# Gathered embeddings plus positions on one core: the first four sequences gathered by halves, with half of the positions and the later indices loaded behind the first half

## The chip, the cores and the metric

The kernel runs on one core of one Trainium2 chip. The metric is the device time of one execution in microseconds (us); lower is better. The program was run several times per measurement, and the median is given. Where a kernel was timed against the kernel before, the two ran alternately on the same chip. Three chips took part in the experiments, and one of them shows a longer closing of the program, which is described where it matters.

## The reference

```python
batch, seq_len, vocab_size, d_model = 32, 512, 50000, 512
def reference(indices, embedding_table, position_embed):
    token_embed = embedding_table[indices]          # (32, 512, 512) float32
    return (token_embed + position_embed).astype(np.float32)
```

There are 16,384 rows of 2 KB to fetch, one position row to add to each, and 33.6 MB to write. Indices come as 64-bit integers.

## The kernel before

A sequence of 512 rows lies on 128 partitions with K = 4 rows each, so a "gather" (one indirect DMA issued from GpSimd) fetches 128 rows, 256 KB. The 128 gathers are numbered by g. VectorE adds the positions, which ScalarE has copied to PSUM, and SyncE stores half sequences (512 KB); the first and the last sequence are stored in quarters.

```python
SLOTS = 24; LANES = 16                       # buffers of a whole sequence; semaphores of gathers
# SyncE: the loads, all issued at once
nc.sync.dma_start(out=idx0[:], in_=idx_first).then_inc(s_first, 16)       # indices of sequence 0: 4 KB
nc.sync.dma_start(out=idx_raw[:], in_=...).then_inc(s_raw, 16)            # all indices: 128 KB
for k in range(K):
    nc.sync.dma_start(out=pos_sb[k][:], in_=pos_rows[:, k, :]).then_inc(s_pos[k], 16)   # 4 x 256 KB
# GpSimd: the gathers
nc.gpsimd.wait_ge(s_first, 16)
for g in range(B * K):
    b, k = divmod(g, K)
    if g == K:
        nc.gpsimd.wait_ge(s_idx, 1)          # later indices, turned by TensorE
    ...
    where = idx0[:, 2 * k : 2 * k + 1] if b == 0 else idx_t[:, k, b : b + 1]
    ins = nc.gpsimd.indirect_dma_start(out=slots[b % SLOTS][:, k, :], out_offset=None,
        in_=table, in_offset=bass.IndirectOffsetOnAxis(ap=where, axis=0),
    ).then_inc(s_gather[g % LANES], 16)
# VectorE: one add for each gather, in the same order; waits for s_gather (and s_ps for b == 0)
# SyncE: stores, each waits for its adds
for b, at, n in stores:
    nc.sync.dma_start(out=out_rows[b][:, at : at + n, :], in_=slots[b % SLOTS][:, at : at + n, :],
    )._wait_ge(s_add, b * K + at + n).then_inc(done, 16)
```

Of the kernel before, what the change touches and what calls it, by code (L numbers as in the profile page):

```python
# [1 line left out]

# [4 lines left out]

P = 128
K = 4
SLOTS = 24  # L10
LANES = 16
HALVES = (2, 2)
QUARTERS = (1, 1, 1, 1)


@with_exitstack
def kernel(
    ctx: ExitStack,
    tc: tile.TileContext,
    indices: bass.AP,  # L20
    embedding_table: bass.AP,
    position_embed: bass.AP,
    out: bass.AP,
):




    nc = tc.nc
    f32 = mybir.dt.float32  # L30
    i32 = mybir.dt.int32
    add = mybir.AluOpType.add

    B, S = indices.shape
    V, D = embedding_table.shape
    assert S == P * K and B == 32
    assert V < (1 << 24), "an index passes through float32"


    idx_words = indices.bitcast(i32)  # L40
    idx_first = idx_words[0].rearrange("(p w) -> p w", p=P)
    out_rows = out.rearrange("b (p k) d -> b p k d", k=K)
    pos_rows = position_embed.rearrange("(p k) d -> p k d", k=K)
    table = embedding_table[:, :]

    def sbuf(name, shape, dtype):
        return ctx.enter_context(tc.tile_pool(name="p_" + name, bufs=1)).tile(
            shape, dtype, name=name
        )

    def psum(name, shape, dtype):
        pool = tc.tile_pool(name="p_" + name, bufs=1, space=bass.MemoryType.PSUM)
        return ctx.enter_context(pool).tile(shape, dtype, name=name)

    idx0 = sbuf("idx0", [P, 2 * K], i32)
    idx_raw = sbuf("idx_raw", [B, S, 2], i32)
    ones = sbuf("ones", [B, B], f32)
    ident = sbuf("ident", [B, B], f32)
    idx_f = sbuf("idx_f", [B, P, K], f32)
    idx_t = sbuf("idx_t", [P, K, B], i32)  # L60
    pos_sb = [sbuf(f"pos_sb{k}", [P, D], f32) for k in range(K)]
    slots = [sbuf(f"slot{n}", [P, K, D], f32) for n in range(SLOTS)]
    turned = psum("turned", [P, K, B], f32)
    pos_ps = [psum(f"pos_ps{k}", [P, D], f32) for k in range(K)]


    stores = []
    for b in range(B):
        parts = QUARTERS if b in (0, B - 1) else HALVES
        at = 0  # L70
        for n in parts:
            stores.append((b, at, n))
            at += n

    sem = tc.alloc_semaphore
    s_first, s_raw = sem("s_first"), sem("s_raw")
    s_pos = [sem(f"s_pos{k}") for k in range(K)]
    s_gather = [sem(f"s_gather{n}") for n in range(LANES)]

    s_out = {b: sem(f"s_out{b}") for b in range(B - SLOTS)}  # L80
    s_rest = sem("s_rest")
    s_ident, s_cast, s_turn, s_idx, s_ps, s_add = (
        sem(n) for n in ("s_ident", "s_cast", "s_turn", "s_idx", "s_ps", "s_add")
    )

    def rounds(g):
        return 16 * (g // LANES + 1)

    with tc.tile_critical(no_gpsimd_drain=True):  # L89

        nc.sync.dma_start(out=idx0[:], in_=idx_first).then_inc(s_first, 16)
        nc.sync.dma_start(
            out=idx_raw[:], in_=idx_words.rearrange("b (s w) -> b s w", w=2)
        ).then_inc(s_raw, 16)
        for k in range(K):
            nc.sync.dma_start(out=pos_sb[k][:], in_=pos_rows[:, k, :]).then_inc(
                s_pos[k], 16
            )


        nc.gpsimd.memset(ones[:], 1.0).then_inc(s_ident, 1)  # L101
        nc.gpsimd.affine_select(  # L102
            out=ident[:], in_=ones[:], pattern=[[-1, B]],
            compare_op=mybir.AluOpType.is_equal, fill=0.0, base=0,
            channel_multiplier=1,
        )._wait_ge(s_ident, 1).then_inc(s_ident, 1)
        nc.gpsimd.wait_ge(s_first, 16)
        for g in range(B * K):
            b, k = divmod(g, K)
            if g == K:  # L110
                nc.gpsimd.wait_ge(s_idx, 1)
            if b >= SLOTS and k == 0:
                done = sum(1 for x in stores if x[0] == b - SLOTS)
                nc.gpsimd.wait_ge(s_out[b - SLOTS], 16 * done)  # L114
            where = idx0[:, 2 * k : 2 * k + 1] if b == 0 else idx_t[:, k, b : b + 1]
            ins = nc.gpsimd.indirect_dma_start(  # L116
                out=slots[b % SLOTS][:, k, :],
                out_offset=None,
                in_=table,
                in_offset=bass.IndirectOffsetOnAxis(ap=where, axis=0),  # L120
            ).then_inc(s_gather[g % LANES], 16)
            if g >= LANES:
                ins._wait_ge(s_gather[g % LANES], rounds(g - LANES))
        nc.gpsimd.drain()  # L124


        nc.tensor.wait_ge(s_ident, 2)
        for k in range(K):
            ins = nc.tensor.transpose(turned[:, k, :], idx_f[:, :, k], ident[:])  # L129
            ins.then_inc(s_turn, 1)  # L130
            if k == 0:
                ins._wait_ge(s_cast, 1)


        nc.vector.tensor_copy(  # L135
            out=idx_f[:].rearrange("b p k -> b (p k)"), in_=idx_raw[:, :, 0]
        )._wait_ge(s_raw, 16).then_inc(s_cast, 1)
        nc.vector.tensor_copy(out=idx_t[:], in_=turned[:])._wait_ge(  # L138
            s_turn, K
        ).then_inc(s_idx, 1)  # L140
        for g in range(B * K):
            b, k = divmod(g, K)
            if b == 0:
                nc.vector.wait_ge(s_ps, k + 1)
            part = slots[b % SLOTS][:, k, :]
            nc.vector.tensor_tensor(  # L146
                out=part, in0=part, in1=pos_ps[k][:], op=add
            )._wait_ge(s_gather[g % LANES], rounds(g)).then_inc(s_add, 1)


        for k in range(K):
            nc.scalar.copy(out=pos_ps[k][:], in_=pos_sb[k][:])._wait_ge(  # L152
                s_pos[k], 16
            ).then_inc(s_ps, 1)
        rest = 0
        for b, at, n in stores:
            done = s_out.get(b, s_rest)
            rest += done is s_rest
            nc.sync.dma_start(
                out=out_rows[b][:, at : at + n, :],  # L160
                in_=slots[b % SLOTS][:, at : at + n, :],
            )._wait_ge(s_add, b * K + at + n).then_inc(done, 16)
        nc.sync.wait_ge(s_rest, 16 * rest)


# [1 line left out]
_INS = ['indices', 'embedding_table', 'position_embed']  # L167
_OUTS = [((32, 512, 512), 'float32')]


# [23 lines left out]
```

## Time and profile before

| quantity | before | where it is read |
|---|---|---|
| time | 177.56 us (177.3 to 177.7, 4 runs) | runs |
| span of the profiled run | 175.4 us | the page |
| bytes moved | 68.33 MB | the page |
| GpSimd's first and last gather issued | 2.88 and 162.23 us | the timeline |
| interval between issues, after the first 30 | 1.2526 us | the timeline |
| last byte moved | 173.18 us | the trace's DMA packets |

The page of the kernel before. The row DMA gives the busy share of the 16 DMA engines in tenths in 40 slices of 4.4 us, GB/s what they moved. A group's line ends with busy time, mean ns of one, idle time and what ended it.

```profile
DMA  3989999999999999999999999999999999999993
GB/s 110 305 251 325 406 405 370 406 398 412 408 407 417 392 419 419 418 419 418 416 419 419 418 417 418 419 417 419 417 417 419 417 419 419 415 413 416 419 413 139
...
L116 POOL DMA_INDIRECT slot<-in_embedding_table_dram,idx_t x124 | 117.5, 948 | 37.8 <-issue 37.8
L146 DVE TENSOR_TENSOR slot<-slot,pos_ps 128x512 f32<-128x512 f32 x128 | 87.8, 687 | 77.1 <-DMA slot<-in_embedding_table_dram,idx_t 72.8
```

From 61 us on, every slice but the last shows 413 to 419 GB/s, about 418 in the mean. That is a gather and an equal share of a store, 524,288 bytes, each 1.2526 us: 418.6 GB/s. So GpSimd's issue rate and the flow of bytes agree. VectorE is idle half of the time.

The waits of the kernel before (who waited for what: us in total, times, longest):

```profile
POOL slot L116 <- issue: 38.7, 127, 0.3
...
POOL slot L116 <- DMA idx<-in_indices_dram: 1.5, 1, 1.5
```

GpSimd waits for no other engine and no buffer after the first indices. "Issue" is 0.30 us between two gathers that nothing in the profile explains.

Windows of the kernel before. The last two columns count: the busy share of the DMA engines, and GB/s. The share is the summed time of the packets that start in the window, over 16 engines, and can come out slightly above 1.

```profile
core 0: us, PE busy (x) PEld busy (x) DVE busy (x) ACT busy (x) POOL busy (x), PEclk, DMA share, GB/s
...
2.50:4.00 1.50, 0.00 (x0) 0.00 (x0) 0.00 (x0) 0.00 (x0) 1.12 (x1) 1.00 0.89 253
4.00:6.00 2.00, 0.68 (x4) 0.55 (x4) 0.70 (x2) 0.59 (x1) 1.39 (x3) 1.00 0.79 215
...
10.00:12.00 2.00, 0.00 (x0) 0.00 (x0) 2.00 (x4) 0.00 (x0) 1.39 (x3) 1.00 0.78 204
12.00:14.00 2.00, 0.00 (x0) 0.00 (x0) 0.81 (x2) 0.00 (x0) 1.70 (x2) 1.00 0.99 358
14.00:16.00 2.00, 0.00 (x0) 0.00 (x0) 0.69 (x1) 0.00 (x0) 1.39 (x3) 1.00 1.02 290
16.00:20.00 4.00, 0.00 (x0) 0.00 (x0) 1.88 (x3) 0.00 (x0) 3.08 (x4) 1.00 0.98 378
20.00:40.00 20.00, 0.00 (x0) 0.00 (x0) 10.39 (x16) 0.00 (x0) 15.12 (x17) 1.00 1.02 395
...
60.00:80.00 20.00, 0.00 (x0) 0.00 (x0) 11.00 (x16) 0.00 (x0) 15.12 (x17) 1.00 1.03 415
...
164.00:168.00 4.00, 0.00 (x0) 0.00 (x0) 2.06 (x3) 0.00 (x0) 0.00 (x0) 1.00 1.03 421
```

The first 20 us move less than the later ones.

The end of the chain of waits (start us, us, what), and the landing times of gathers issued from 80 to 160 us:

```profile
162.23 7.47 DMA slot<-in_embedding_table_dram,idx_t
169.70 0.02 issue
169.72 0.69 DVE slot L146
```

```profile
DMA to landing us min/median/max: 6.9/7.3/7.8
```

A gather takes 7.3 us to land in mid-run and 7.47 us at the end. The shortest landing in this trace is 4.4 us. The last add comes at 169.72 us, and the last byte at 173.18 us, 10.96 us after GpSimd's last issue.

The first add:

```profile
9.50 2.63 DVE L146 TENSOR_TENSOR slot<-slot,pos_ps 128x512 f32<-128x512 f32 x4 [3.93 <-DMA slot<-in_embedding_table_dram,idx]
```

### The profile page before, as it was taken

Reading aid. Unit: us, or ns where it says so; the run is one execution under the profiler, and the core shown is the slowest. Engines: PE = TensorE matmul, PEld = TensorE weight load, DVE = VectorE, ACT = ScalarE, POOL = GpSimd, SP = SyncE. Lnnn points to the kernel's source line nnn. Section 1 sums busy time; section 2 is a strip of 40 time slices with the busy share of each in tenths; the row PEclk is TensorE's granted clock in tenths of the full one; section 3 lists DMA queues with packets and bytes.
Section 4 is the critical chain, followed back from the end, with each engine's and each line's share of the span. In section 5 each row is a group of like instructions: output and inputs, shape, how many; then the busy total and the mean of one; then the engine's idle time right before and its main releaser. Section 6 shows DMA issues by size and latency. Waiting matters only on the chain.

```text
span 175.4 us, 421 instructions
## 1 busy us (share of the span) xinstructions
PE 0.7 (0%) x4; PEld 0.6 (0%) x4; DVE 88.5 (50%) x130; ACT 3.6 (2%) x5; POOL 122.1 (70%) x134
## 2 busy tenths in 40 slices
PE   0100000000000000000000000000000000000000
PEld 0100000000000000000000000000000000000000
DVE  0072564564646455554655555555554546556440
ACT  2410000000000000000000000000000000000000
POOL 3777777777777777777777777777777777777200
DMA  3989999999999999999999999999999999999993
GB/s 110 305 251 325 406 405 370 406 398 412 408 407 417 392 419 419 418 419 418 416 419 419 418 417 418 419 417 419 417 417 419 417 419 419 415 413 416 419 413 139
DMA packets 20803, 68.33 MB, mean 390 GB/s; under 512 B 3360, under 2 KB 3360, under 8 KB 20800
## 3 DMA queue, kind: packets, MB, share of 16 engines
q1 hardware_dynamic: 10560, 34.74, 49.4%
q0 software_dynamic: 10240, 33.56, 49.1%
q14 instruction: 3, 0.02, 0.1%
HBM read 34.74 MB, written 33.55 MB: 389 GB/s over the span
## 4 chain that ended last, share of the span: by engine, by line
POOL 67%; issue 24%; DMA 5%; POOLq 1%; DVE 0%; SPq 0%
POOL slot L116 67%; DMA slot<-in_embedding_table_dram,idx_t 4%; DMA idx<-in_indices_dram 1%; POOLq L124 1%; DVE slot L146 0%; POOLq L114 0%; SPq L189 0%; SPq L89 0%
## 5 line engine op out<-in xcount | busy, mean ns | idle before, releaser
L116 POOL DMA_INDIRECT slot<-in_embedding_table_dram,idx_t x124 | 117.5, 948 | 37.8 <-issue 37.8
L146 DVE TENSOR_TENSOR slot<-slot,pos_ps 128x512 f32<-128x512 f32 x128 | 87.8, 687 | 77.1 <-DMA slot<-in_embedding_table_dram,idx_t 72.8
L116 POOL DMA_INDIRECT slot<-in_embedding_table_dram,idx x4 | 4.0, 1009 | 2.4 <-DMA idx<-in_indices_dram 1.5
L135 DVE CAST idx_f<-idx_raw 32x512 f32<-32x512 int32 x1 | 0.4, 414 | 4.1 <-DMA idx_raw<-in_indices_dram 4.1
L152 ACT COPY pos_ps<-pos_sb 128x512 f32<-128x512 f32 x4 | 2.4, 589 | 4.8 <-DMA pos_sb<-in_position_embed_dram 4.6
L152 ACT ACT_TABLE_LOAD x1 | 1.3, 1283 | 1.0 <-SPq L89 1.0
L129 PE MATMUL turned<-ident,idx_f 32*128 32x32 f32 x4 | 0.7, 308 | 4.6 <-DVE idx_f L135 4.6
L138 DVE CAST idx_t<-turned 128x128 int32<-128x128 f32 x1 | 0.3, 291 | 0.8 <-PE turned L129 0.8
L129 PEld LDWEIGHTS turned<-ident,idx_f 32*128 32x128 f32 x4 | 0.6, 206 | 4.6 <-DVE idx_f L135 4.6
L101 POOL MEMSET ones<- 32x32 f32 x1 | 0.1, 115 | 0.5 <-SPq L89 0.5
L178 POOL MEMSET const-float32-0.0<- 128x1 f32 x1 | 0.1, 105 | 0.3 <-issue 0.3
L102 POOL TENSOR_SCALAR_AFFINE_SELECT ident<-ones 32x32 f32<-32x32 f32 x1 | 0.2, 203 | 0.1
L178 POOL MEMSET const-uint8-127<- 128x1 uint8 x1 | 0.1, 122 | 0.0
L178 POOL MEMSET const-bfloat16-1.0<- 128x1 bf16 x1 | 0.1, 116 | 0.0
L178 POOL MEMSET const-float32-1.0<- 128x1 f32 x1 | 0.1, 108 | 0.0
## 6 DMA issues: line engine op xcount, KB each, us to landing
out_dram<-slot SPq DMA_DIRECT2D x60, 512.0 KB, 6.7
out_dram<-slot SPq DMA_DIRECT2D x8, 256.0 KB, 4.3
slot<-in_embedding_table_dram,idx_t POOLq DMA_INDIRECT x124, 7.2
pos_sb<-in_position_embed_dram SPq DMA_DIRECT2D x4, 256.0 KB, 5.2
idx_raw<-in_indices_dram SPq DMA_DIRECT2D x1, 128.0 KB, 2.6
slot<-in_embedding_table_dram,idx POOLq DMA_INDIRECT x4, 5.5
idx<-in_indices_dram SPq DMA_DIRECT2D x1, 4.0 KB, 1.6
```

The source lines that it names most:

```text
L101: nc.gpsimd.memset(ones[:], 1.0).then_inc(s_ident, 1)
L102: nc.gpsimd.affine_select(out=ident[:], in_=ones[:], pattern=[[-1, B]], compare_op=mybir.AluOpType.is_equal, fill=0.0, base=0, channel_mul ...
L116: ins = nc.gpsimd.indirect_dma_start(out=slots[b % SLOTS][:, k, :], out_offset=None, in_=table, in_offset=bass.IndirectOffsetOnAxis(ap=whe ...
L124: nc.gpsimd.drain()
L129: ins = nc.tensor.transpose(turned[:, k, :], idx_f[:, :, k], ident[:])
L135: nc.vector.tensor_copy(out=idx_f[:].rearrange("b p k -> b (p k)"), in_=idx_raw[:, :, 0])._wait_ge(s_raw, 16).then_inc(s_cast, 1)
L138: nc.vector.tensor_copy(out=idx_t[:], in_=turned[:])._wait_ge(s_turn, K).then_inc(s_idx, 1)
L146: nc.vector.tensor_tensor(out=part, in0=part, in1=pos_ps[k][:], op=add)._wait_ge(s_gather[g % LANES], rounds(g)).then_inc(s_add, 1)
L152: nc.scalar.copy(out=pos_ps[k][:], in_=pos_sb[k][:])._wait_ge(s_pos[k], 16).then_inc(s_ps, 1)
L178: nc = _bacc.Bacc("TRN2", target_bir_lowering=False, num_devices=1)
```

## The change

The intent is a better start: the first stores should begin sooner and the DMA engines should not be lopsided. The first four sequences are gathered by their first halves (eight gathers that need only the first half of the positions), then by their second halves. The second half of the positions and the full load of indices are issued behind a wait for the first half. The first load of indices covers four sequences. The later indices are loaded on 128 partitions, so the identity for the turning is 128 wide and the turned indices are copied in four parts. One buffer fewer fits (23).

```diff
-SLOTS = 24
+SLOTS = 23
+FIRST = 4
+Q = 32
-    idx_first = idx_words[0].rearrange("(p w) -> p w", p=P)
+    idx_first = idx_words[0:FIRST].rearrange("b (p w) -> p b w", p=P)
+    half = K // 2
+    order = [(b, k) for h in range(2) for b in range(FIRST)
+             for k in range(h * half, (h + 1) * half)]
+    order += [(b, k) for b in range(FIRST, B) for k in range(K)]
         nc.sync.dma_start(out=idx0[:], in_=idx_first).then_inc(s_first, 16)
+        load_pos(0)
+        nc.sync.wait_ge(s_pos[0], 16)
+        load_pos(1)
         nc.sync.dma_start(
-            out=idx_raw[:], in_=idx_words.rearrange("b (s w) -> b s w", w=2)
+            out=idx_raw[:], in_=idx_rows.rearrange("r (s w) -> r s w", w=2)
         ).then_inc(s_raw, 16)
-        for k in range(K):
-            nc.sync.dma_start(out=pos_sb[k][:], ...
-            if g == K:
-                nc.gpsimd.wait_ge(s_idx, 1)
+            if g == FIRST * K:
+                nc.gpsimd.wait_ge(s_idx, J)
# ... cut: tiles as one [P, K, D] instead of four [P, D]; VectorE casts the later indices at g == 7
# ... and copies the turned ones at g == 9; stores follow the new order
```

More of the change, by code (lines that the diff above doesn't have):

```diff
@@ L9 @@
 K = 4
-SLOTS = 24
+SLOTS = 23
 LANES = 16
-HALVES = (2, 2)
-QUARTERS = (1, 1, 1, 1)
+FIRST = 4
+Q = 32
 @with_exitstack
@@ L37 @@
     assert V < (1 << 24), "an index passes through float32"
+    J = P // Q
     idx_words = indices.bitcast(i32)
-    idx_first = idx_words[0].rearrange("(p w) -> p w", p=P)
+    idx_first = idx_words[0:FIRST].rearrange("b (p w) -> p b w", p=P)
+    idx_rows = idx_words.rearrange("b (j w) -> (b j) w", j=J)
     out_rows = out.rearrange("b (p k) d -> b p k d", k=K)
@@ L53, in psum @@
         return ctx.enter_context(pool).tile(shape, dtype, name=name)
-    idx0 = sbuf("idx0", [P, 2 * K], i32)
-    idx_raw = sbuf("idx_raw", [B, S, 2], i32)
-    ones = sbuf("ones", [B, B], f32)
-    ident = sbuf("ident", [B, B], f32)
-    idx_f = sbuf("idx_f", [B, P, K], f32)
+    idx0 = sbuf("idx0", [P, FIRST, 2 * K], i32)
+    idx_raw = sbuf("idx_raw", [P, Q * K, 2], i32)
+    ones = sbuf("ones", [P, P], f32)
+    ident = sbuf("ident", [P, P], f32)
+    idx_f = sbuf("idx_f", [P, Q, K], f32)
     idx_t = sbuf("idx_t", [P, K, B], i32)
-    pos_sb = [sbuf(f"pos_sb{k}", [P, D], f32) for k in range(K)]
+    pos_sb = sbuf("pos_sb", [P, K, D], f32)
     slots = [sbuf(f"slot{n}", [P, K, D], f32) for n in range(SLOTS)]
-    turned = psum("turned", [P, K, B], f32)
-    pos_ps = [psum(f"pos_ps{k}", [P, D], f32) for k in range(K)]
-    stores = []
-    for b in range(B):
-        parts = QUARTERS if b in (0, B - 1) else HALVES
-        at = 0
-        for n in parts:
-            stores.append((b, at, n))
-            at += n
+    turned = psum("turned", [Q, K, B, J], f32)
+    pos_ps = psum("pos_ps", [P, K, D], f32)
+    half = K // 2
+    order = [(b, k) for h in range(2) for b in range(FIRST)
+             for k in range(h * half, (h + 1) * half)]
+    order += [(b, k) for b in range(FIRST, B) for k in range(K)]
+    stores = []
+    for g, (b, k) in enumerate(order):
+        if (b == 0 and k < half) or b == B - 1:
+            stores.append((g + 1, b, k, 1))
+        elif k % half == half - 1:
+            stores.append((g + 1, b, k + 1 - half, half))
     sem = tc.alloc_semaphore
     s_first, s_raw = sem("s_first"), sem("s_raw")
-    s_pos = [sem(f"s_pos{k}") for k in range(K)]
+    s_pos = [sem(f"s_pos{h}") for h in range(2)]
     s_gather = [sem(f"s_gather{n}") for n in range(LANES)]
@@ L87, in rounds, with load_pos @@
         return 16 * (g // LANES + 1)
+    def load_pos(h):
+        at = slice(h * half, (h + 1) * half)
+        nc.sync.dma_start(out=pos_sb[:, at, :], in_=pos_rows[:, at, :]).then_inc(
+            s_pos[h], 16
+        )
     with tc.tile_critical(no_gpsimd_drain=True):
         nc.sync.dma_start(out=idx0[:], in_=idx_first).then_inc(s_first, 16)
+        load_pos(0)
+        nc.sync.wait_ge(s_pos[0], 16)
+        load_pos(1)
         nc.sync.dma_start(
-            out=idx_raw[:], in_=idx_words.rearrange("b (s w) -> b s w", w=2)
+            out=idx_raw[:], in_=idx_rows.rearrange("r (s w) -> r s w", w=2)
         ).then_inc(s_raw, 16)
-        for k in range(K):
-            nc.sync.dma_start(out=pos_sb[k][:], in_=pos_rows[:, k, :]).then_inc(
-                s_pos[k], 16
-            )
         nc.gpsimd.memset(ones[:], 1.0).then_inc(s_ident, 1)
         nc.gpsimd.affine_select(
-            out=ident[:], in_=ones[:], pattern=[[-1, B]],
+            out=ident[:], in_=ones[:], pattern=[[-1, P]],
             compare_op=mybir.AluOpType.is_equal, fill=0.0, base=0,
@@ L107 @@
         nc.gpsimd.wait_ge(s_first, 16)
-        for g in range(B * K):
-            b, k = divmod(g, K)
-            if g == K:
-                nc.gpsimd.wait_ge(s_idx, 1)
+        for g, (b, k) in enumerate(order):
+            if g == FIRST * K:
+                nc.gpsimd.wait_ge(s_idx, J)
             if b >= SLOTS and k == 0:
-                done = sum(1 for x in stores if x[0] == b - SLOTS)
+                done = sum(1 for x in stores if x[1] == b - SLOTS)
                 nc.gpsimd.wait_ge(s_out[b - SLOTS], 16 * done)
-            where = idx0[:, 2 * k : 2 * k + 1] if b == 0 else idx_t[:, k, b : b + 1]
+            if b < FIRST:
+                where = idx0[:, b, 2 * k : 2 * k + 1]
+            else:
+                where = idx_t[:, k, b : b + 1]
             ins = nc.gpsimd.indirect_dma_start(
@@ L128 @@
         for k in range(K):
-            ins = nc.tensor.transpose(turned[:, k, :], idx_f[:, :, k], ident[:])
+            ins = nc.tensor.transpose(
+                turned[:, k].rearrange("p b j -> p (b j)"), idx_f[:, :, k], ident[:]
+            )
             ins.then_inc(s_turn, 1)
@@ L132 @@
                 ins._wait_ge(s_cast, 1)
-        nc.vector.tensor_copy(
-            out=idx_f[:].rearrange("b p k -> b (p k)"), in_=idx_raw[:, :, 0]
-        )._wait_ge(s_raw, 16).then_inc(s_cast, 1)
-        nc.vector.tensor_copy(out=idx_t[:], in_=turned[:])._wait_ge(
-            s_turn, K
-        ).then_inc(s_idx, 1)
-        for g in range(B * K):
-            b, k = divmod(g, K)
+        for g, (b, k) in enumerate(order):
+            if g == 7:
+                nc.vector.tensor_copy(
+                    out=idx_f[:].rearrange("r p k -> r (p k)"), in_=idx_raw[:, :, 0]
+                )._wait_ge(s_raw, 16).then_inc(s_cast, 1)
+            if g == 9:
+                nc.vector.wait_ge(s_turn, K)
+                for j in range(J):
+                    nc.vector.tensor_copy(
+                        out=idx_t[j * Q : (j + 1) * Q, :, :], in_=turned[:, :, :, j]
+                    ).then_inc(s_idx, 1)
             if b == 0:
@@ L146 @@
             nc.vector.tensor_tensor(
-                out=part, in0=part, in1=pos_ps[k][:], op=add
+                out=part, in0=part, in1=pos_ps[:, k, :], op=add
             )._wait_ge(s_gather[g % LANES], rounds(g)).then_inc(s_add, 1)
         for k in range(K):
-            nc.scalar.copy(out=pos_ps[k][:], in_=pos_sb[k][:])._wait_ge(
-                s_pos[k], 16
+            nc.scalar.copy(out=pos_ps[:, k, :], in_=pos_sb[:, k, :])._wait_ge(
+                s_pos[k // half], 16
             ).then_inc(s_ps, 1)
         rest = 0
-        for b, at, n in stores:
+        for adds, b, at, n in stores:
             done = s_out.get(b, s_rest)
@@ L161 @@
                 in_=slots[b % SLOTS][:, at : at + n, :],
-            )._wait_ge(s_add, b * K + at + n).then_inc(done, 16)
+            )._wait_ge(s_add, adds).then_inc(done, 16)
         nc.sync.wait_ge(s_rest, 16 * rest)
```

## The prediction

> **What bounds the kernel now.** Two rates coincide. The timeline shows GpSimd issuing a gather (256 KB) every 1.253 us, 0.95 us of work and 0.30 us of "issue", from 2.88 to 163.2 us; the waits view gives it no wait but 1.5 us for the first indices. A gather and its share of a store are 512 KB in 1.253 us, 418 GB/s. The DMA engines deliver no more when full: the page's slices settle at 417 to 419 GB/s, and the windows from 164 to 168 us, after the last gather was issued, show 421. So the 68.3 MB need 163.5 us; the span is 175.4 us. By the windows, 7.2 of the 12 us lost are lost in the first 20 us (2.5 us before any bulk data), some 1.7 us from 20 to 60 us (378 to 415 GB/s), 3 us in the tail. Backlog from the poor start stays: gathers land 4.4 us after issue at best, 7.2 us in the median, 7.5 us at the end. The Trainium skill, "DMA: Bandwidth & Descriptors", section "Issuing engines are not separate DMA queues", says that all issuers share 16 engines and interleave; the trace agrees: the first gather takes 6.6 us to land beside 1 MB of positions and 128 KB of indices.
>
> **What the change does.** It works on the start only.
> - Taken from ahead of the first gather: the late indices and half the positions. I expect the first 512 KB of positions to land near 5 us, the first gather near 7.5 us instead of 9.47, the first store issued near 8.3 us instead of 10.21.
> - Order: the first eight gathers need only half 0 of the positions, so half 1 and the indices (issued near 5 us, landing near 7.5 us) hold nobody up. 10 to 12 us (204 GB/s, gathers alone) should be near full rate.
> - Added: the first index load has 512 pieces of 32 bytes, not 128; it landed after 1.58 us, I estimate 0.3 to 0.6 us more, and GpSimd's whole chain shifts by that. A new hole of about 1 us between the end of half 0 (about 4.3 us) and the first gather's packets. Wider identity, four copies of turned indices: 1 to 2 us of work in slack (DVE adds take 0.69 of each 1.25 us; late indices are first needed near 23 us). 23 slots: that wait ended long before.
>
> **How much counts.** Only DMA time not lost. By 10 us I expect no gain (less to move, plus the hole); from 10 to 17 us about 1.7 us. But stores still follow gathers at GpSimd's pace, and with less backlog the stretch to 60 us should leak somewhat more. GpSimd's last issue comes 0.3 to 0.6 us later; the gain can only be a shorter landing of the last gathers (7.5 us to about 5.5) and stores. Net estimate: 1.5 us.
>
> **Prediction.** 176.1 us, range 174.7 to 177.6. Faster by over 2%: 0.08; within 2%: 0.90; slower by over 2%: 0.02.
>
> **Right if:** the first store issue is near 8.3 us; 10 to 12 us exceeds 330 GB/s; mid-run gathers land in under 6.7 us; GpSimd still issues every 1.253 us without waits, ending 0.3 to 0.6 us later; the time from its last issue to the end shrinks by about 2 us.
>
> **Wrong if:** backlog grows back to 7.3 us by mid-run, since both rates are equal (no gain, even 0.4 us loss); the wider index load is much slower; the wait between the halves empties the DMA longer; or earlier stores keep the engines full throughout (174 us).

## The result, and the profile after

| quantity | before | after |
|---|---|---|
| time, first comparison | 177.56 us (177.3 to 177.7, 4 runs) | 176.98 us (176.73 to 177.2, 4 runs) |
| ratio, 95% interval | | 0.9969, 0.9948 to 0.9989 |
| first indices landed | 2.60 us | 3.03 us |
| first gather issued, landed | 2.88, 9.47 us | 3.31, 6.76 us |
| first and second store issued | 10.21, 10.87 us | 7.50, 11.57 us |
| last gather issued | 162.23 us | 162.31 us |
| last byte moved | 173.18 us | 173.15 us |
| span of the profiled run | 175.4 us | 175.5 us |

A ratio is the mean time of one kernel's fast runs over that of the other's of the same rounds, so it is not quite the ratio of the medians. The gain is 0.3%, 0.56 us between the means; 1.5 us were forecast. The prediction was wrong in size, and the two profiled runs hardly differ at their ends. That 176.98 us lies inside the predicted range says little, for the range holds the time of the kernel before as well.

The page after:

```profile
DMA  4799999999999999999999999999999999999993
GB/s 120 234 316 309 349 383 402 390 410 410 416 412 418 416 419 419 418 418 418 416 421 418 420 418 420 418 418 419 418 416 417 420 418 418 418 419 418 418 413 130
...
L131 POOL DMA_INDIRECT slot<-in_embedding_table_dram,idx_t x112 | 105.9, 946 | 34.1 <-issue 34.1
L166 DVE TENSOR_TENSOR slot<-slot,pos_ps 128x512 f32<-128x512 f32 x128 | 87.9, 688 | 81.5 <-DMA slot<-in_embedding_table_dram,idx_t 63.6
```

Windows after, in the columns shown for before:

```profile
2.50:4.00 1.50, 0.00 (x0) 0.00 (x0) 0.00 (x0) 0.00 (x0) 0.69 (x1) 1.00 0.89 285
4.00:6.00 2.00, 0.00 (x0) 0.00 (x0) 0.00 (x0) 0.97 (x2) 1.40 (x2) 1.00 0.48 147
...
10.00:12.00 2.00, 0.00 (x0) 0.00 (x0) 0.69 (x1) 0.68 (x2) 1.65 (x2) 1.00 0.96 315
12.00:14.00 2.00, 0.00 (x0) 0.00 (x0) 1.12 (x2) 0.42 (x1) 1.44 (x2) 1.00 0.92 312
14.00:16.00 2.00, 0.00 (x0) 0.00 (x0) 1.48 (x3) 0.00 (x0) 1.40 (x2) 1.00 0.97 306
16.00:20.00 4.00, 1.04 (x4) 0.44 (x4) 2.04 (x4) 0.00 (x0) 3.08 (x4) 1.00 0.94 337
20.00:40.00 20.00, 0.00 (x0) 0.00 (x0) 11.51 (x20) 0.00 (x0) 15.12 (x17) 1.00 1.02 392
...
60.00:80.00 20.00, 0.00 (x0) 0.00 (x0) 11.13 (x17) 0.00 (x0) 15.13 (x17) 1.00 1.03 419
...
164.00:168.00 4.00, 0.00 (x0) 0.00 (x0) 2.29 (x4) 0.00 (x0) 0.00 (x0) 1.00 1.03 421
```

The hole that the wait makes is there: from 4 to 6 us the engines are busy 0.48 of the time, 0.79 before. From 10 to 12 us 315 GB/s move instead of 204, but from 12 to 14 us it is 312 after 358, from 14 to 16 us 306 after 290, and from 16 to 20 us 337 after 378. Over the whole of the first 20 us the change moved no more than before (258 GB/s after 268). From 60 us on both kernels run at GpSimd's pace.

The first two adds after:

```profile
6.79 0.69 DVE L166 TENSOR_TENSOR slot<-slot,pos_ps 128x512 f32<-128x512 f32 x1 [6.79 <-DMA slot<-in_embedding_table_dram,idx]
10.85 0.69 DVE L166 TENSOR_TENSOR slot<-slot,pos_ps 128x512 f32<-128x512 f32 x1 [3.37 <-DMA slot<-in_embedding_table_dram,idx]
```

The first gather lands 2.7 us earlier than before. The second one lands 4 us after it: it shares the DMA engines with the second half of the positions (experiment 3 tests this), which was issued at 5.02 us and landed at 11.30 us, not near 7.5 us as predicted.

The end of the chain after, and the landing times from 80 to 160 us:

```profile
162.31 7.63 DMA slot<-in_embedding_table_dram,idx_t
169.94 0.02 issue
169.96 0.69 DVE slot L166
```

```profile
DMA to landing us min/median/max: 7.0/7.4/7.8
```

Gathers land in 7.4 us in mid-run and in 7.63 us at the end. This is the predicted failure, "backlog grows back to 7.3 us by mid-run".

### The profile page after: what moved, and what is told of

It is laid out like the page before. It is cut to its first block, busy times and chain, and to the rows that moved or that the text cites. A ratio compares the mean times of both kernels' runs of the same rounds, so it can differ in the third digit from the quotient of the medians.

```text
span 175.5 us, 423 instructions
## 1 busy us (share of the span) xinstructions
PE 1.0 (1%) x4; PEld 0.4 (0%) x4; DVE 89.1 (51%) x133; ACT 3.5 (2%) x5; POOL 121.9 (69%) x134
## 4 chain that ended last, share of the span: by engine, by line
POOL 66%; issue 24%; DMA 5%; POOLq 1%; DVE 0%; SPq 0%
POOL slot L131 66%; DMA slot<-in_embedding_table_dram,idx_t 4%; DMA idx<-in_indices_dram 1%; POOLq L139 1%; DVE slot L166 0%; POOLq L126 0%; SPq L211 0%; SPq L103 0%
## 5 line engine op out<-in xcount | busy, mean ns | idle before, releaser
L131 POOL DMA_INDIRECT slot<-in_embedding_table_dram,idx_t x112 | 105.9, 946 | 34.1 <-issue 34.1
L131 POOL DMA_INDIRECT slot<-in_embedding_table_dram,idx x16 | 15.3, 958 | 6.3 <-issue 4.6
L160 DVE CAST idx_t<-turned 32x128 int32<-32x128 f32 x4 | 1.1, 279 | 0.1
L144 PE MATMUL turned<-ident,idx_f 128*32 128x128 f32 x4 | 1.0, 416 | 17.2 <-DVE idx_f L154 17.2
```

The source lines that it names most:

```text
L144: ins = nc.tensor.transpose(turned[:, k].rearrange("p b j -> p (b j)"), idx_f[:, :, k], ident[:])
L160: nc.vector.tensor_copy(out=idx_t[j * Q : (j + 1) * Q, :, :], in_=turned[:, :, :, j]).then_inc(s_idx, 1)
```

## The experiments

Two theories stood against each other.

- **Theory A:** the DMA engines' total work is the bound from start to end. Bytes or idle time saved anywhere come off the time; the change gained little because its hole ate most of what it saved.
- **Theory B:** GpSimd's pace is the bound, and the number of bytes waiting settles at the same level whatever the start was. The end is GpSimd's start, plus 127 intervals, plus a tail that depends only on the settled level.

One note for the first eight experiments. On their chip the kernel before takes 183.5 us. The bytes are done at the same time as elsewhere (172.4 to 174.1 us), but the span ends 8 to 10 us after the last byte instead of 2.2 us: some of SyncE's closing instructions there take 0.7 or 1.4 us each instead of 0.03 or less. All these spans but that of experiment 7 end near 182 us, although the last bytes differ by 1.7 us, so a gain of that size can be hidden on that chip. The cause was not found. For these runs the time of the last byte, from one profile each, is given too.

### 1. The change again

No edit.

> The change once more, five rounds on one chip with the kernel before, because the first result (0.3% faster) is no larger than the spread of single runs. Both theories: 0.1 to 0.5% faster than before. First load of indices lands near 3.0 us, GpSimd's first gather near 3.3 us, mid-run gathers land 7.0 to 7.5 us after issue.

183.56 us against 183.51; ratio 1.0001 (0.9985 to 1.0017). First indices and first gather came as expected (3.17 us). Last byte at 173.92 us. The gain did not show on this chip. Gathers settled at 8.5 us from issue to add (the add starts within some hundredths of a microsecond of the landing), where 7.0 to 7.5 us were expected.

### 2. No load of the positions

```diff
 # the kernel before
-        for k in range(K):
-            nc.sync.dma_start(out=pos_sb[k][:], in_=pos_rows[:, k, :]).then_inc(s_pos[k], 16)
+        for k in range(K):                        # on VectorE, ahead of its other work
+            nc.vector.memset(pos_sb[k][:], 0.0).then_inc(s_pos[k], 1)
```

> The kernel before with the 1 MB of positions not loaded but set to zero on chip (result wrong on purpose); GpSimd's issues are untouched. Theory A (the DMA engines are the bound from start to end, so a byte saved at the start is a time saved at the end): 1.05 MB at 418 GB/s is 2.5 us, so 1.8 to 2.6 us (1.0 to 1.5%) faster. Theory B (GpSimd's pace is the bound, the backlog grows back to a landing time near 7.3 us whatever the start was): within 0.3 us of before, mid-run gathers again at 7.3 us.

182.91 us against 183.51; ratio 0.9971 (0.9958 to 0.9984), 0.5 us where Theory A asks for 1.8 to 2.6 and Theory B for at most 0.3. Its output is wrong, which doesn't matter for the time. Because the slow closing might have hidden a gain, it was run again later on a chip without it.

> The kernel before with the positions set to zero instead of loaded (wrong on purpose), again, in the hope of a chip without the slow closing, which may have hidden part of a gain. Theory A: 1.8 to 2.6 us faster. Theory B: 0 to 0.7 us faster.

177.41 us against 177.25; ratio 1.0015 (0.9991 to 1.0040). A whole megabyte taken out of the start bought nothing. Windows of this run:

```profile
2.50:4.00 1.50, 0.00 (x0) 0.00 (x0) 0.86 (x3) 1.50 (x4) 0.97 (x1) 1.00 0.34 87
...
6.00:8.00 2.00, 0.00 (x0) 0.00 (x0) 0.69 (x2) 0.00 (x0) 1.62 (x2) 1.00 0.77 176
...
14.00:16.00 2.00, 0.00 (x0) 0.00 (x0) 1.41 (x3) 0.00 (x0) 1.39 (x3) 1.00 1.00 349
...
80.00:100.00 20.00, 0.00 (x0) 0.00 (x0) 10.94 (x16) 0.00 (x0) 15.13 (x17) 1.00 1.03 417
```

The early windows are emptier than before (87 GB/s from 2.5 to 4 us, before 253; 176 from 6 to 8, before 356), and the engines have idle time. Over the first 60 us this run moved 342 GB/s and the first trace of before 358, about 1 MB less: no other traffic took the place of the saved megabyte. From 80 us on it is 417 GB/s again, and the last byte moves at 173.83 us. From a gather's issue to the start of its add it took 6.3 us for those issued from 20 to 30 us, 7.8 from 50 to 60, 8.5 from 130 us on. Theory A is refuted for the start.

### 3. The change without its wait

```diff
 # the change
-        nc.sync.wait_ge(s_pos[0], 16)
```

> The change without the wait on the first half of the positions: the second half and the later indices are issued at once behind the first half. Theory A: the hole that the wait opens in the DMA (0.48 busy from 4 to 6 us, about 1 us idle) closes, and second half and gathers no longer collide at 6 to 9 us: 0.5 to 1.0 us faster than the change. Theory B: same as the change within 0.2 us.

183.69 us against 183.51; ratio 1.0012 (0.9999 to 1.0026). No gain from closing the hole shows, though this chip could hide a small one. The last byte came at 172.65 us in this one profile; in four profiles of the unchanged change it came at 173.15, 173.92, 174.06 and 173.70 us, so this is no proof of a gain, and experiment 9 finds none. The run also tests the collision: here the second half landed at 6.52 us, and the second add started at 8.83 us, 1.3 us behind the first instead of 4.

### 4. Gathers from 8 MB of the table

Gather packets of 4 KB normally take 159 ns. Counted in the trace, 9.7% of them in the first 20 us of before took over 250 ns, 3.2% from 20 to 40 us, 0.1% after 60 us. These stretched packets explain in good part how the engines can be busy at 290 GB/s: in the window from 14 to 16 us they took 0.70 of the 2.05 us of each engine's packet time. The first guess was that parts of the table are touched for the first time.

```diff
 # the kernel before, on VectorE: idx0 and the later indices
+ tensor_single_scalar(out=..., in_=..., scalar=4095, op=bitwise_and)
```

> The kernel before with every index cut to its low 12 bits on the vector engine (result wrong on purpose), so that the gathers read 8 MB of the table instead of 102 MB; bytes and issues are the same, GpSimd starts about 0.3 us later. Theory A, with its part on slow packets (gather packets over 250 ns, 7 to 17% of the first 512 and under 0.1% after 60 us, cost 3 us of every engine's time because they touch parts of the table for the first time): slow packets fall by more than half, 10 to 12 us moves more than 204 GB/s, and the time falls by 1 to 3 us. If slow packets are as many as before, first touches are not their cause. Theory B: 0.0 to 0.4 us slower, whatever the packets do.

183.72 us against 183.51; ratio 1.0015 (1.0002 to 1.0028). Stretched packets were as many as before (8.7% and 6.2% in the first two stretches of 20 us). First touches are not their cause; this part of Theory A fell. GpSimd started at 3.13 us instead of 2.88, and the run was 0.2 us slower, as Theory B has it, though this chip's closing could have hidden part of a gain.

### 5. The change with a narrow first load

```diff
 # the change
-        nc.sync.dma_start(out=idx0[:], in_=idx_first).then_inc(s_first, 16)
+        nc.sync.dma_start(out=idx0[:, 0, :], in_=idx_first[:, 0, :]).then_inc(s_first, 16)
+        nc.sync.dma_start(out=idx0[:, 1:, :], in_=idx_first[:, 1:, :]).then_inc(s_more, 16)
+            if g == half:
+                nc.gpsimd.wait_ge(s_more, 16)
```

> The change, with the first load of indices cut to the first sequence's 4 KB as before, and the other three sequences' indices in a second small load behind it. GpSimd's first gather should start 0.3 to 0.4 us earlier than in the change (near 2.9 us). Theory B (the end is GpSimd's start, plus 127 intervals, plus a tail that is always alike): 0.3 to 0.4 us faster than the change. Theory A (the DMA engines' total work): within 0.15 us of the change.

183.32 us, the change beside it 183.25 (experiment 8), before 183.49. The first gather started at 2.97 us. The times do not tell the theories apart on this chip; the last byte was at 172.36 us against 174.06 in the change, in one profile each, whose settled gaps from issue to add (7.2 and 8.3 us) differ too. It was run on two other chips, below.

### 6. Stores left out in mid-run

```diff
 # the kernel before, when the list of stores is made
-            stores.append((b, at, n))
+            if not (8 <= b < SLOTS and at):
+                stores.append((b, at, n))
```

> The kernel before without the store of the second half of sequences 8 to 23 (result wrong on purpose): 16 of 68 stores, 8.4 MB, are missing between about 45 and 125 us. Theory A: 8.4 MB at 418 GB/s is 20 us faster. Theory B: GpSimd ends at the same time, 162 us; with fewer stores, gathers land in about 5 us from 50 to 120 us. After 125 us the full load is back for 38 us: if the DMA delivers less than 418 GB/s while its queues are short, the landing time climbs again to 7 us before the end, slow packets come back on the way, and the time is within 1.5 us of before; if not, landing stays near 5 us and the run is 2 to 3.5 us faster.

183.76 us against 183.49; ratio 1.0014 (0.9998 to 1.0029). 8.4 MB fewer bytes, and nothing gained. The output is incomplete. Windows of this run:

```profile
100.00:120.00 20.00, 0.00 (x0) 0.00 (x0) 10.87 (x17) 0.00 (x0) 15.12 (x17) 1.00 0.94 312
130.00:135.00 5.00, 0.00 (x0) 0.00 (x0) 1.97 (x3) 0.00 (x0) 3.78 (x5) 1.00 0.92 302
...
140.00:150.00 10.00, 0.00 (x0) 0.00 (x0) 5.47 (x8) 0.00 (x0) 7.56 (x9) 1.00 1.02 398
150.00:160.00 10.00, 0.00 (x0) 0.00 (x0) 5.32 (x8) 0.00 (x0) 7.56 (x9) 1.00 1.02 408
```

GpSimd's busy time, 15.12 us in 20, is that of the kernel before, and its interval stayed at 1.252 to 1.253 us: less traffic does not make it issue faster, so the DMA does not set its pace. With a quarter of the demand missing, 312 GB/s flow while the engines still show 0.94 busy. When the stores come back after 126 us, the engines first deliver only 302 GB/s. The following table, worked out from the trace, shows the gap from a gather's issue to the start of its add, and the share of stretched gather packets:

| gathers issued from, us | 40 to 50 | 100 to 110 | 120 to 130 | 130 to 140 | 140 to 150 | 150 to 160 |
|---|---|---|---|---|---|---|
| issue to add, us | 7.0 | 5.0 | 5.2 | 6.4 | 6.8 | 7.1 |
| gather packets over 250 ns | 0.4% | 13.3% | 10.3% | 9.1% | 3.2% | 1.4% |

Short queues bring the stretched packets back in the middle of the run, and both vanish together as the queues fill. So stretched packets belong to short queues, not to the start of the program. While the queues are short, the DMA delivers less than it is asked for, and the backlog grows until the delivery meets GpSimd's pace. It took some 30 us here, and the last byte moved at 172.99 us.

### 7. One small memset after each gather

```diff
 # the kernel before
+            nc.gpsimd.memset(tick[:, g : g + 1], 0.0)
```

> The kernel before with one tiny memset on GpSimd after each gather, which makes its interval longer by some 0.05 to 0.15 us. Theory A: DMA work is unchanged, so less than 2 us slower. Theory B: slower by 127 times the added interval (6 to 19 us), less 2 to 3 us of shorter tail, because demand is now below what the DMA delivers and gathers land in about 5 us all along. Slow packets: if they belong to short queues, they go on through the whole run; if they belong to a cold start, they are gone after 60 us as before.

191.25 us against 183.49; ratio 1.0417 (1.0401 to 1.0433). The experiment did not do what it was made for: the memset of 0.09 us fits into the 0.30 us gap, and the median interval stayed at 1.251 us. But GpSimd was held up near 47, 89, 129 and 162 us, by 3 to 5 us each time and in steps of 0.7 us, for a reason that the trace does not show; the slow closing of other runs on this chip has the same 0.7 us steps. Its last gather was issued at 178.75 us, 16.5 us later than in before, and the last byte moved at 188.01 us. The closing took 2.2 us in this run, which is why the time grew by 7.8 us only. The stops are a test in themselves: the gap from issue to add was 7.3 us before the first stop and fell to 5.2 us after it; after the second stop it fell from 7.2 to 3.8 us and was back at 7.9 us 12 us later. After each of the first three stops the gap was above 7 us again within 13 us of the stop's end, though it swung for a while; after the last it had reached 6.8 us when the gathers ended. Stretched packets came back after the stops, with all stores in place: from 64 to 68 us gathers and stores moved 0.58 MB each, and 21.8% of the gather packets were stretched. So the missing stores of experiment 6 are not what stretches them. Of the 16.5 us that GpSimd lost, 14.8 come out at the last byte.

### 8. The change once more beside these

> The change unchanged, on the same chip as the other three, to compare the narrow first load with: 0 to 0.5% faster than before; first gather near 3.2 to 3.3 us; GpSimd's interval near 1.2505 us against 1.2525 us in before.

183.25 us against 183.49; ratio 0.9983 (0.9970 to 0.9997). GpSimd's interval was 1.2534 us, where the same kernel on the same chip had 1.2504 us in experiment 1. The interval is not a property of the kernel. Nor is the settled gap from issue to add: 8.4 us here, 7.3 to 7.7 us in the first trace of the change.

### 9. Narrow first load and no wait

> The change with the narrow first load and without the wait between the halves of the positions, as a version that should beat both. Theory B: only GpSimd's start counts, so 0.3 to 0.4 us faster than the change, like the narrow load alone, and 0 to 0.6 us faster than before. Theory A: the filled hole (1 us idle) comes on top, 1.0 us or more faster than the change. If the chip shows the slow closing again (8 to 10 us from the last byte to the end of the span, as in all earlier experiments but the slower pace), the time of the last byte decides: 173.1 us in the change.

The edits of experiments 3 and 5 together: 177.29 us against 177.25; ratio 1.0007 (0.9984 to 1.0029). The closing was normal (2.35 us). Filling the hole gave nothing, and this version is not faster than before. The 0.3 us of the earlier start did not show either: GpSimd's interval was 1.2529 us in this run. Beside the narrow version with the wait on the same chip (experiment 11) it is 0.7 us slower, and the two intervals of the ratio do not overlap; Theory B had the two alike. GpSimd's interval makes 0.3 us of that in the profiled runs (1.2529 after 1.2502 us); the rest is not explained.

### 10. Stores left out late

```diff
 # the kernel before, when the list of stores is made
+            if not (23 <= b < B - 1 and at):
```

> The kernel before without the store of the second half of sequences 23 to 30 (result wrong on purpose): 8 stores, 4.2 MB, missing between about 123 and 162 us, so that the queues are short when GpSimd ends. Theory A: 10 us faster. Theory B: GpSimd ends as before; the last gathers land in 4.5 to 5.5 us instead of 7.5, and the last byte moves from 10.9 us after GpSimd's last issue to 7.5 to 9 us: 2 to 3.4 us faster, unless the slow closing hides it.

174.00 us against 177.25; ratio 0.9810 (0.9788 to 0.9832). The output is incomplete. Theory A asked for 10 us, Theory B for 2 to 3.4; it is 3.25. GpSimd's last gather was issued at 162.43 us. Windows of this run:

```profile
100.00:120.00 20.00, 0.00 (x0) 0.00 (x0) 10.74 (x16) 0.00 (x0) 15.13 (x17) 1.00 1.03 417
...
140.00:160.00 20.00, 0.00 (x0) 0.00 (x0) 11.56 (x18) 0.00 (x0) 15.12 (x17) 1.00 0.98 332
```

The last gathers needed 5.3 us from issue to add, and the last byte came 7.8 us after GpSimd's last issue instead of 10.9. Half as many bytes left out as in experiment 6 gain 3.25 us instead of nothing, because they leave the queues short at the end. The position in time decides, not the number of bytes. Of the 3.1 us by which the last byte follows GpSimd's last issue sooner, 2.1 are the landing of the last gather (5.34 us, in the first trace of before 7.47); how much of the rest is due to the left-out stores themselves was not separated.

### 11. The narrow first load on a chip with a normal closing

> The change with the narrow first load again, for the same reason. Theory B: 0.3 to 0.4 us faster than the change, so 0.3 to 1.0 us faster than before.

176.55 us against 177.25; ratio 0.9967 (0.9951 to 0.9983). The first gather was issued at 2.89 us.

### 12. What makes up the 0.3%

Four kernels were run beside each other on a third chip.

> The kernel before itself, for a second trace of it and for the noise of a comparison of a kernel with itself: ratio 1.000 within 0.2%. GpSimd's first gather 2.88 us; if its interval is 1.2526 us again and the settled landing 7.3 us, both belong to the kernel; if not, they differ from run to run.

> The change on the same chip: 0.0 to 0.5% faster than before. First gather 3.2 to 3.3 us, last byte 10.4 to 11.8 us after GpSimd's last issue.

> The kernel before with the change's wide first load (16 KB in 512 pieces) and nothing else: the one part of the change that costs. Theory B: GpSimd starts 0.3 to 0.4 us later and the run is 0.2 to 0.5 us slower than before. Theory A: no difference.

> The change with the narrow first load, beside the change on the same chip: 0.2 to 0.5 us faster than the change, 0.4 to 0.9 us faster than before.

The edit of e15 puts the change's 16 KB first load into the kernel before and nothing else:

```diff
-    idx_first = idx_words[0].rearrange("(p w) -> p w", p=P)
+    idx_first = idx_words[0:4].rearrange("b (p w) -> p b w", p=P)
```

| kernel | time, us | ratio to before (95%) | first gather | interval after 30, us | last gather | last byte |
|---|---|---|---|---|---|---|
| before (e13) | 177.45 | 1.0006 (0.9983 to 1.0029) | 3.09 | 1.2504 | 162.05 | 173.28 |
| change (e14) | 177.15 | 0.9986 (0.9955 to 1.0018) | 3.18 | 1.2502 | 162.16 | 173.70 |
| before, wide first load (e15) | 177.42 | 1.0009 (0.9982 to 1.0036) | 3.18 | 1.2504 | 162.20 | 173.32 |
| change, narrow first load (e16) | 176.81 | 0.9966 (0.9939 to 0.9992) | 2.89 | 1.2504 | 161.87 | 173.60 |

Before itself had an interval of 1.2504 us this time and 1.2526 in its first trace: 127 of these 2.2 ns are 0.28 us, a run-to-run difference as large as the gain that was to be explained. The wide first load cost less than the runs scatter, where Theory B expected 0.2 to 0.5 us; but the first gather of before came at 3.09 us here instead of 2.88, so that the load delayed it by 0.09 us only and the test says little. The change is between 0.0 and 0.3% faster in four comparisons (0.9969, 1.0001, 0.9983, 0.9986), and only two of these intervals leave out 1. The narrow version is 0.3% faster than before in both of its comparisons with a normal closing. Beside the change it is 0.34 us faster by the medians, but the two intervals overlap.

## Why the prediction was right or wrong

- **The bound: half right.** The two rates do coincide, and GpSimd never waits. But the sentence "Only DMA time not lost", the answer to "How much counts", is wrong. Experiments 2 and 6 took 1 and 8.4 MB away and the time stayed. DMA time saved in the first 126 us gains nothing here, because GpSimd's pace, which did not change when bytes were left out, holds the demand down, and the queue refills before the end.
- **The early landmarks: right.** The first half of the positions landed at 5.00 us (near 5 predicted), the first gather at 6.76 us (7.5), the first store was issued at 7.50 us (8.3), the hole in the DMA is there (0.48 busy from 4 to 6 us), and GpSimd started 0.43 us later (0.3 to 0.6).
- **Half 1 of the positions: wrong.** It was to "hold nobody up". It landed at 11.30 us and made the second gather land 4 us behind the first, so the second store was issued later than before (11.57 after 10.87 us).
- **10 to 12 us near full rate: wrong in size.** 315 GB/s, where over 330 was asked for; the engines were 0.96 busy. The prediction took the 204 GB/s of before as room to fill, but the engines were 0.78 busy there. With short queues the same bytes occupy the engines longer. The Trainium skill, "Perfetto Trace Analysis", section "Identifying the Most-Contended Engine", says to judge the DMA by HBM utilization instead of occupancy, because 16 engines make occupancy misleading; the trace agrees (0.94 busy at 312 GB/s in experiment 6), and adds that GB/s alone misleads about the idle room.
- **The step that failed.** It is the path from the start to the end: "from 10 to 17 us about 1.7 us" of DMA time was to be gained, and then "the gain can only be a shorter landing of the last gathers (7.5 us to about 5.5) and stores. Net estimate: 1.5 us." The early gain hardly came: from 10 to 17 us the change moved 303 GB/s and before 286, which is 0.3 us at 418 GB/s. Over the first 20 us it moved 258 GB/s in its first profile and 265 to 269 in three later ones, the kernel before 268 and 261. Nor would it have lasted. The last gather landed in 7.63 us, not 5.5, and the last byte came 10.84 us after GpSimd's last issue, not some 9. The prediction let a shorter backlog last from 20 us to 162 us with only some leak up to 60 us, and gave "backlog grows back" only as a risk. The experiments show that refilling takes some 9 to 30 us (experiments 6 and 7), and that even a whole megabyte saved at the start leaves nothing at the end of a run of 160 us (experiment 2). Only a short queue at the very end is worth something: 3.25 us for 5.3 us from issue to add (experiment 10, which also has fewer bytes left to move then).
- **GpSimd's end.** It came 0.08 us later instead of 0.3 to 0.6, mostly since its interval was 2.1 ns shorter in that run. That is luck and not the change: the change also ran at 1.2534 us (experiment 8), and before at 1.2504 (experiment 12).
- **What stays open.** Why packets stretch while queues are short was not settled; that they do is shown, and a cold table is ruled out as the main cause. The settled level differs between runs of one kernel (narrow version: 7.3 us from issue to add on one chip, 8.5 on another), and GpSimd's interval lies near one of two values (1.2502 to 1.2505 or 1.2526 to 1.2534 us); neither cause was found. The level weighs more than the edits of the start: over the 16 traces other than those of experiments 7 and 10, GpSimd's last issue came within 0.7 us (161.9 to 162.5), the last add started 7.2 to 8.6 us after it, and the last byte moved 3.1 to 3.5 us after that. So the 0.0 to 0.3% of the change is not taken apart further. No run made GpSimd faster, so how much a shorter interval would gain was not shown.

## What to carry to other kernels

Where an engine issues work at a fixed pace that nearly equals what the DMA delivers, as here, a better or worse start can be forgotten within some tens of microseconds: look for gains at the issuing engine's start, at its interval and in the last queue's length before the end. The interval alone promises little here, since the demand of 418.6 GB/s is close to the most that was seen (420 GB/s over 10 us). Test a supposed DMA bound by leaving bytes out in different parts of the run before building anything for it. A low GB/s beside a high busy share does not mean idle engines (312 GB/s at 0.94 busy in experiment 6), and it is not their limit either: with longer queues the same engines moved 408 GB/s.

## What the Trainium skill lacked or had wrong

- "DMA: Bandwidth & Descriptors", section "Anatomy of one DMA — SWDGE (gpsimd) path", gives one DMA's time as about 2.0 us plus bytes over 436 GB/s, which is 2.6 us for 256 KB as an estimate from that formula. It gives no landing time for a stream of DMAs that runs near the limit: here the same 256 KB landed 3.5 us after issue in the first gather of the change, 7.3 us in mid-run, 5.0 to 5.3 us with a quarter fewer bytes asked for (issue to add), and returned to 7 us when the stores came back.
- The same page has no word on packets stretching when queues are short: 0.4% of the 4 KB gather packets took over 250 ns with full queues (40 to 50 us in experiment 6), about 12% with short ones (80 to 120 us) in the same run.
- "Perfetto Trace Analysis", section "Roofline", puts a single core's ceiling at its 16 DMA engines, about 435 GB/s. No stretch of 10 us in the 18 traces moved more than 420 GB/s, and none of 4 us more than about 425.
- No page has the indirect gather's issue interval, which bounds this kernel: 0.946 or 0.949 us of work and 0.30 us of gap for 128 rows, 1.2504 or 1.2526 us in all.
- No page has a closing like the one on one of the chips: some of SyncE's last instructions took 0.7 or 1.4 us each, and the span ended 8 to 10 us after the last byte instead of 2.2 us.
